# Output projection of a hybrid block on one Trainium2 core: products 6, 7 and 4 accumulate in product 1's PSUM banks, and the transposes between the products move

## The chip, the cores and the metric

The kernel runs on one core of one Trainium2 chip. A core has five engines with a queue each: TensorE (PE in the profile, its weight loads PEld), VectorE (DVE), ScalarE (ACT), GpSimd (POOL) and SyncE (SP, which here only issues DMAs). The engines work in their own order and wait for each other by semaphores. The metric is the device time of one execution in microseconds; the program is compared by the median of several.

## The reference

One layer of a streaming encoder on 512 tokens of 1024 channels: a gated linear attention and a forgetting attention side by side, a gated merge, an output projection with a residual, a gated MLP with a short causal convolution, and a last norm. The part that the change touches is the merge's projection and the norm behind it:

```python
y = sigmoid(g_gla + gate_b[0]) * (o_gla @ w_gla_branch) \
    + sigmoid(g_fox + gate_b[1]) * (o_fox @ w_fox_branch)
x = x + y @ w_out                       # (512, 1024) @ (1024, 1024)
a, val = split(rmsnorm(x, norm_ffn_g) @ w_up, 2)
a = causal_dwconv(a, conv_w, conv_b)
x = x + (gelu(a) * val) @ w_down
return rmsnorm(x, norm_final_g)
```

All of it is float32.

## The kernel before

**Products.** Each float32 product is three TensorE matmuls on rounded parts (`mm3`, L314 to L316: high by high, low by high, high by low). Every weight piece (128 x 1024) is loaded, cast by ScalarE to its high part (`wh`, L280) and subtracted by VectorE to its low part (`wl`, L281), some pieces ahead of TensorE; there are three buffers for each part, so a cast waits until TensorE has left the piece three places back.

**The output projection** `y @ w_out` is done in a Strassen-like scheme: seven products on quarters, each 256 tokens by 512 channels, two weight pieces (r = 0, 1) and 24 matmuls of 128x512. A product fills two PSUM banks, one for each 128 tokens. The order is `OUT`: 1, 5, 2, 3, 6, 7, 4. `out_product` (L1137) issues one. Some weight pieces are sums of blocks: pieces of 6, 7 and 4 arise in place, by accumulating DMAs that GpSimd issues (L288) into the pieces of 5, 3 and 6 as soon as VectorE's split of those has read them. Their tiles are called `zr` (5, 6, 4) and `rawz` (3, 7).

The residual rows `x2[tt][j]` (`x2t` in the profile; tt is the 128-token tile, j the half of the channels) are loaded from x and take the results: `finish_block` (L1151) adds or subtracts two banks (L1154), has ScalarE square the row block for the norm (L1156) and stores it (L1157). Product 1 enters four blocks of the result. It is accumulated with product 2 in its own banks for block (0, 0), and before that copied to SBUF (`ox`, L1200); GpSimd applies the copy to the three other blocks with six additions of 128x512 (L1210). Products 6, 7 and 4 then accumulate in two fresh banks `accy`, which are read after each of them: after 6 for block (0, 1), after 7 for (1, 1), after 4 for (1, 0). Each reading must be over before the next product adds to the bank.

**Transposes.** The MLP wants x by channels. `transpose_half(0)` (L1172, eight 128x128 transposes into two banks) turns block (0, 0) and stands between products 3 and 6; `transpose_later` (L1190, sixteen into four banks) turns blocks (0, 1) and (1, 1) and stands between the two weight pieces of product 4; `transpose_half(1)` stands later, within the first plain MLP products. ScalarE copies the banks out with a scale (L1177, L1191) and casts (L1181, L1192), VectorE subtracts (L1182, L1193).

**Behind the projection** come the first plain products of the up projection (L1234), the sum of squares (L1253), an inverse square root on VectorE (L348 to L358), its spreading over the partitions by TensorE (L412), ScalarE's copy of that (L416) and VectorE's scaling of x (L1297), on which the up projection rests.

The order of an engine's instructions is fixed when the program is built: a scheduler places the recorded instructions by their dependencies, and each queue then runs strictly in that order. PSUM has eight banks in two pools of four, `ps_mm` and `ps_ax`.

Of the kernel before, what the change touches and what calls it, by code (L numbers as in the profile page):

```python
# [9 lines left out]
F32 = mybir.dt.float32  # L10
# [3 lines left out]
AF = mybir.ActivationFunctionType  # L14
# [6 lines left out]
NT = T // P  # L21
D = 1024
KD = D // P
# [10 lines left out]
C_MIX, C_FFN, C_AB, C_OG, C_GB, C_CW, C_CB, C_FB, C_QG, C_KG = 0, 8, 16, 18, 22, 38, 104, 126, 127, 128  # L34
# [16 lines left out]
NCL = 2  # L51
# [30 lines left out]
def hybrid_kernel(ctx: ExitStack, tc, xT, xt, wp, wu, wd, wf, pp, aw2, fing, out):  # L82
    nc = tc.nc
# [218 lines left out]
    def piece():  # L302
        n = taken[0]
        taken[0] += 1
        while len(splits) < min(NP, n + NW + sum(i in spare for i in range(n, n + NW))):
            split_next()
            load_ahead(len(splits))
            for i, b, c in copies_at.get(len(splits) - 1, ()):
                with tc.issue_after(last_load[0].ins):
                    nc.sync.dma_start(wsum[i][:, c], b[:, c])  # L310
        return splits[n]

    def mm3(ps, ah, al, bh, bl, start, stop, **k):
        mm(ps, lhsT=ah, rhs=bh, start=start, stop=False, **k)  # L314
        mm(ps, lhsT=ah, rhs=bl, start=False, stop=False, **k)  # L315
        mm(ps, lhsT=al, rhs=bh, start=False, stop=stop, **k)  # L316
# [62 lines left out]
    def col(c, rows=P):  # L379
        return ppt[:rows, c : c + 1]  # L380
# [5 lines left out]
        out=negm, in_=negm, pattern=[[-1, P]], base=0, channel_multiplier=1, compare_op=ALU.is_ge, fill=-1e30  # L386
# [5 lines left out]
        out=gmask, in_=gmask, pattern=[[1, P]], base=0, channel_multiplier=-1, compare_op=ALU.is_ge, fill=0.0  # L392
# [71 lines left out]
    first = [pmm(), pmm(), pmm(), pmm(), pax()]  # L464
# [16 lines left out]
    for k in range(KD):  # L481
        nc.scalar.activation(out=xh[k], in_=xrs[k], func=AF.Copy, scale=col(C_MIX + k))  # L482
        split_next()
        with tc.issue_after(first_copy[0].ins):
            nc.vector.scalar_tensor_tensor(
                out=xl[k], in0=xrs[k], scalar=col(C_MIX + k), in1=xh[k].bitcast(F32),
# [13 lines left out]
    def last_first(products):  # L500
# [17 lines left out]
        out=gqs, in0=col(C_QG), scalar=FD ** -0.5, in1=col(C_KG), op0=ALU.mult, op1=ALU.mult  # L518
# [32 lines left out]
    for j in range(2):  # L551
# [4 lines left out]
            out=mz[:, j, :], in0=pz, scalar1=col(C_AB + j), scalar2=0.0, op0=ALU.add, op1=ALU.min  # L556
# [11 lines left out]
        out=bz.rearrange("p a b -> p (a b)"), data0=rmask, data1=mz.rearrange("p a b -> p (a b)"),  # L568
# [4 lines left out]
        out=fm, data0=ones[:FH, 0:1].broadcast_to([FH, T]), data1=ft, initial=0.0, op0=ALU.mult, op1=ALU.add,  # L573
# [173 lines left out]
    for j in range(2):  # L747
        pt = pax()
# [29 lines left out]
    for tt in range(NT):  # L778
# [45 lines left out]
    for u in range(2):  # L824
# [251 lines left out]
    for h in range(GH):  # L1076
# [4 lines left out]
            out=zr[h], in0=ogr[h], scalar=col(C_OG + h), in1=zr[h], op0=ALU.mult, op1=ALU.mult  # L1081
# [6 lines left out]
    for c in range(-GAHEAD, KD):  # L1088
# [23 lines left out]
        else:  # L1112
            k = c - KD // 2
# [15 lines left out]
    x2 = [[opool.tile([P, T], F32, tag="ot", name="x2t", bufs=2 * GH) for _ in range(2)] for _ in range(NT)]  # L1129
# [3 lines left out]
    xs = x2pool.tile([P, 2 * KB * H], F32, tag="act2", name="xs")[:, : KD * T].rearrange("p (k t) -> p k t", t=T)  # L1133
    x2h, x2l = xh, xl
    ssq = cpool.tile([P, NT, 2], F32, name="ssq")

    def out_product(p, accs, rs=(0, 1), first=True):  # L1137
        (oh, ol), t0 = oops[p]
        for r in rs:
            wh, wl = held[r] if p == 1 else piece()  # L1140
            for t2 in range(2):
                t = slice(t0 + t2 * P, t0 + (t2 + 1) * P)
                for j in range(2):
                    k = 2 * r + j
                    c = slice(j * 512, (j + 1) * 512)
                    mm3(
                        accs[t2], oh[k][:, t], ol[k][:, t], wh[:, c], wl[:, c], first and k == 0, k == KD // 2 - 1,
                        skip_group_check=not first,
                    )

    def finish_block(i, j, accs, op):  # L1151
        for t2 in range(2):
            x = x2[2 * i + t2][j]
            op(out=x, in0=x, in1=accs[t2])  # L1154
            junk = bpool.tile([P, T], F32, tag="zf", name="junk", bufs=GAHEAD + 1)
            nc.scalar.activation(out=junk, in_=x, func=AF.Square, accum_out=ssq[:, 2 * i + t2, j : j + 1])  # L1156
            nc.scalar.dma_start(x2d[:, 2 * i + t2, j * T : (j + 1) * T], x)  # L1157
# [23 lines left out]
            nc.scalar.copy(out=x2k[0], in_=xs[:, k : k + 2, t])  # L1181
            nc.vector.tensor_sub(out=x2k[1], in0=xs[:, k : k + 2, t], in1=x2k[0].bitcast(F32))  # L1182

    def transpose_later():

        for k in range(KD // 2, KD):
            pt = pax()
            for tt in range(NT):
                c = (k - KD // 2) * P
                nc.tensor.transpose(pt[:, tt * P : (tt + 1) * P], x2[tt][1][:, c : c + P], ident)  # L1190
            nc.scalar.activation(out=xs[:, k], in_=pt, func=AF.Copy, scale=col(C_FFN + k))  # L1191
            nc.scalar.copy(out=x2h[k], in_=xs[:, k])  # L1192
            nc.vector.tensor_sub(out=x2l[k], in0=xs[:, k], in1=x2h[k].bitcast(F32))  # L1193

    accx = [pmm(), pmm()]
    out_product(1, accx)
    ox = []
    for t2 in range(2):
        ox.append(bpool.tile([P, T], F32, tag="sg", name="ox", bufs=2))
        nc.scalar.copy(out=ox[t2], in_=accx[t2])  # L1200
    accz = [pmm(), pmm()]
    out_product(5, accz)
    for t2 in range(2):
        x = x2[2 + t2][1]
        nc.vector.tensor_sub(out=x, in0=x, in1=accz[t2])
    out_product(2, accx, first=False)
    finish_block(0, 0, accx, nc.vector.tensor_add)
    for t2 in range(2):
        for tt, j, op in ((t2, 1, nc.gpsimd.tensor_sub), (2 + t2, 1, nc.gpsimd.tensor_sub), (2 + t2, 0, nc.gpsimd.tensor_add)):
            op(out=x2[tt][j], in0=x2[tt][j], in1=ox[t2])  # L1210
    out_product(3, accz, first=False)
    for t2 in range(2):
        x = x2[t2][1]
        nc.vector.tensor_sub(out=x, in0=x, in1=accz[t2])
    transpose_half(0)
    accy = [pmm(), pmm()]
    out_product(6, accy)
    finish_block(0, 1, accy, nc.vector.tensor_sub)
    out_product(7, accy, first=False)
    finish_block(1, 1, accy, nc.vector.tensor_sub)  # L1220
    out_product(4, accy, rs=(0,), first=False)
    transpose_later()
    out_product(4, accy, rs=(1,), first=False)
    finish_block(1, 0, accy, nc.vector.tensor_add)

# [2 lines left out]
    plain = []  # L1228
# [4 lines left out]
            for ps, (wh, wl) in zip(banks, ws):  # L1233
                mm3(ps, wh[:, c], wl[:, c], x2h[k], x2l[k], k == k0, k == k1)  # L1234

    plain.append((pmm(), pmm()))
    up = (piece(), piece())
    later = range(KD // 2, KD)
    plain_products(plain[0][:1], up[:1], later, later[0], -1)
# [67 lines left out]
    nc.vector.tensor_sub(out=y1, in0=x22, in1=x21)  # L1307
    split_x(5, y1)
    minus_sum(y2, y1, x11)
    plain.append((pmm(), pmm()))  # L1310
    up = (piece(), piece())
    plain_products(plain[1], up, range(KD))
    scale_x(x12, 0)
# [110 lines left out]
    for n, (g, p) in enumerate(steps):  # L1424
# [5 lines left out]
        first = name not in st  # L1430
# [15 lines left out]
        elif p == 4:  # L1446
# [5 lines left out]
            for i, c in enumerate((st["x"], ps)):  # L1452
                for j, k, fs in parts:
                    nc.vector.tensor_mul(
                        out=act[j][:, i, k], in0=halves(c)[:, fs], in1=t0[:, fs, i * H : (i + 1) * H]
# [232 lines left out]
```

## Time and profile before

| | |
|---|---|
| median of 3 runs | 713.47 us (712.8 to 716.25) |
| the profiled execution | 714.62 us |
| its span, first to last instruction | 712.9 us |
| mean granted TensorE clock | 0.992 |
| output projection, products 1 to 4 on TensorE | 324.6 to 373.5 us of the span |

All rows below are from the one profiled execution; their times are in microseconds from the start of its span. A row of the timeline gives start, duration, engine, line, operation, output and inputs, shapes, a count where equal neighbours are merged, and in brackets how long the engine had been idle before and what ended that. Matmul rows overlap, so a matmul's cost is the distance to the next one's start. A row of waits gives the total, the number of times and the longest. The window rows give for a stretch the busy time of each engine with counts, the granted clock as a share of the full one, and how full the DMA engines were.

### The profile page before, as it was taken

How to read it: one execution, taken by the hardware profiler on the slowest of the kernel's cores; microseconds unless marked ns; L12 is line 12 of the kernel's file. 1: busy time of each engine (PE TensorE's matmuls, PEld its weight loads, DVE VectorE, ACT ScalarE, POOL GpSimd, SP SyncE). 2: the span in 40 equal slices, each digit the busy share in tenths (PEclk: the TensorE clock that was granted, in tenths of full speed). 3: DMA queues.
4: the chain of work that ended last, by engine and by line, in shares of the span. 5: the costliest groups of instructions: out<-in, count | busy, mean ns of one | idle time of the engine just before them, and what ended most of it. 6: DMA issues, size and time to landing. Idle time of an engine off the chain costs nothing.

```text
span 712.9 us, 11200 instructions
## 1 busy us (share of the span) xinstructions
PE 695.3 (98%) x4130; PEld 606.2 (85%) x4130; DVE 561.8 (79%) x843; ACT 435.8 (61%) x699; POOL 201.7 (28%) x248
## 2 busy tenths in 40 slices
PE   8999999999999999999899999999999999999996
PEld 6887788787887788888678999999999999888875
DVE  6874888977767675686658998888888889987984
ACT  6487665687967843344556756555565566655653
POOL 6215010225533324335500132243434311000222
PEclk9999999999999999999989999999999999999998
DMA  9658478876666389977747587777777887766643
GB/s 328 252 174 293 96 247 226 294 167 171 163 171 156 90 223 214 264 158 207 160 166 231 124 202 173 168 186 176 188 176 182 205 196 221 269 217 176 192 134 118
DMA packets 44742, 138.19 MB, mean 194 GB/s; under 512 B 5240, under 2 KB 8328, under 8 KB 44560
## 3 DMA queue, kind: packets, MB, share of 16 engines
q1 hardware_dynamic: 30864, 92.85, 38.0%
q0 software_dynamic: 10656, 39.33, 31.0%
q10 hardware_dynamic: 3168, 5.31, 2.1%
q8 instruction: 32, 0.52, 0.3%
q14 instruction: 22, 0.18, 0.1%
HBM read 133.25 MB, written 27.28 MB: 225 GB/s over the span
## 4 chain that ended last, share of the span: by engine, by line
PE 76%; DVE 9%; ACT 5%; DMA 4%; issue 4%; POOL 2%; ACTq 0%; DVEq 0%; POOLq 0%
PE ps_mm L314 18%; PE ps_mm L316 17%; PE ps_mm L315 17%; PE ps_ax L315 6%; PE ps_ax L316 6%; PE ps_ax L314 6%; DVE wl L281 2%; DMA zr<-in_wp_dram 1%; DMA cb<-nct 1%; POOL x2t L1210 1%; DMA rawx<-wsum 1%; DVE ln L949 1%; ACT pr L962 1%; PE ps_pt L971 1%; ACT pr L955 1%
## 5 line engine op out<-in xcount | busy, mean ns | idle before, releaser
L314 PE MATMUL ps_mm<-xh,wh 128*128 128x512 f32 (+1 forms) x312 | 107.4, 346 | 1.2 <-DVE wh L276 0.8
L280 ACT CAST wh<-rawx 128x1024 fp32r<-128x1024 f32 x75 | 76.1, 1014 | 52.4 <-PE ps_mm L315 24.0
L316 PE MATMUL ps_mm<-xh,wl 128*128 128x512 f32 (+1 forms) x312 | 106.6, 343 | 0.0
L315 PE MATMUL ps_mm<-xl,wh 128*128 128x512 f32 (+1 forms) x312 | 106.4, 342 | 0.0
L281 DVE TENSOR_TENSOR wl<-rawx,wh 128x1024 fp32r<-128x1024 f32 x75 | 88.9, 1190 | 14.5 <-ACT wh L280 14.4
L281 DVE TENSOR_TENSOR wl<-raw,wh 128x1024 fp32r<-128x1024 f32 x58 | 78.1, 1349 | 9.1 <-ACT wh L280 8.8
L280 ACT CAST wh<-raw 128x1024 fp32r<-128x1024 f32 x58 | 60.5, 1047 | 28.9 <-PE ps_mm L315 20.4
L314 PEld LDWEIGHTS ps_mm<-xh,wh 128*128 128x128 f32 x312 | 59.1, 190 | 8.3 <-ACT xh L482 1.7
L316 PEld LDWEIGHTS ps_mm<-xh,wl 128*128 128x128 f32 x312 | 59.2, 190 | 7.7 <-DVE wl L277 0.7
L315 PEld LDWEIGHTS ps_mm<-xl,wh 128*128 128x128 f32 x312 | 59.3, 190 | 5.9
L288 POOL DMA_DIRECT2D rawx<-in_wu_dram x30 | 26.1, 869 | 111.2 <-DVE wl L281 106.3
L281 DVE TENSOR_TENSOR wl<-rawz,wh 128x1024 fp32r<-128x1024 f32 x31 | 41.3, 1336 | 18.0 <-ACT wh L280 17.9
L254 POOL TENSOR_TENSOR rawx<-rawx,raw 128x256 f32<-128x256 f32 x32 | 38.2, 1221 | 27.7 <-DMA rawx<-in_wu_dram 27.7
L314 PE MATMUL ps_mm<-xo,wh 128*128 128x256 f32 x160 | 45.5, 284 | 0.0
L315 PE MATMUL ps_mm<-xo,wh 128*128 128x256 f32 x160 | 45.3, 283 | 0.0
L316 PE MATMUL ps_mm<-xo,wl 128*128 128x256 f32 x160 | 45.3, 283 | 0.0
L1331 DVE SCALAR_TENSOR_TENSOR t<-ap,ppt,t 128x512 f32<-128x512 f32 x44 | 43.9, 1051 | 0.0
L280 ACT CAST wh<-rawz 128x1024 fp32r<-128x1024 f32 x31 | 32.4, 1046 | 17.3 <-DMA rawz<-in_wp_dram 6.6
L314 PE MATMUL ps_mm<-wh,xh 128*128 128x512 f32 x108 | 42.8, 398 | 0.1
L314 PE MATMUL ps_mm<-xc,wh 128*128 128x256 f32 (+1 forms) x128 | 42.5, 332 | 0.0
L315 PE MATMUL ps_mm<-xc,wh 128*128 128x256 f32 (+1 forms) x128 | 42.5, 332 | 0.0
L316 PE MATMUL ps_mm<-xc,wl 128*128 128x256 f32 (+1 forms) x128 | 42.4, 331 | 0.0
(471 smaller groups left out, 2046.7 us busy)
## 6 DMA issues: line engine op xcount, KB each, us to landing
rawx<-in_wu_dram POOLq DMA_DIRECT2D x32, 512.0 KB, 6.3
rawz<-in_wp_dram SPq DMA_DIRECT2D x30, 512.0 KB, 5.3
raw<-in_wp_dram SPq DMA_DIRECT2D x22, 512.0 KB, 6.2
wsum<-in_wd_dram SPq DMA_DIRECT2D x20, 512.0 KB, 6.6
rawx<-in_wu_dram SPq DMA_DIRECT2D x20, 512.0 KB, 6.0
raw<-in_wu_dram SPq DMA_DIRECT2D x20, 512.0 KB, 4.6
rawx<-wsum SPq DMA_DIRECT2D x12, 512.0 KB, 4.3
wsum<-in_wd_dram POOLq DMA_DIRECT2D x10, 512.0 KB, 8.6
```

What stands on the lines that cost most here:

```text
L254: nc.gpsimd.tensor_add(out=raws[n][:, c], in0=raws[n][:, c], in1=raws[other][:, c])
L280: nc.scalar.copy(out=hi[:, :m], in_=raw[:, :m])
L281: nc.vector.tensor_sub(out=lo[:, :m], in0=raw[:, :m], in1=hi[:, :m].bitcast(F32))
L288: added[:] = [nc.gpsimd.dma_start(raw, recipes[i][0], accum_op=ALU.add)]
L314: mm(ps, lhsT=ah, rhs=bh, start=start, stop=False, **k)
L315: mm(ps, lhsT=ah, rhs=bl, start=False, stop=False, **k)
L316: mm(ps, lhsT=al, rhs=bh, start=False, stop=stop, **k)
L949: nc.vector.tensor_tensor_reduce(out=ln[:, :n], in0=lg[:, :n], in1=cb[:, CBO[qb] : CBO[qb] + n], scale=-1.0, scalar=3e38, op0=ALU.add, op1 ...
L955: last_exp = nc.scalar.activation(out=pr[:, :n], in_=ln[:, :n], func=AF.Exp, scale=-1.0, bias=nm, accum_out=rs)
L962: nc.scalar.activation(out=pr[:, :n], in_=pr[:, :n], func=AF.Copy, scale=rs)
L971: nc.tensor.transpose(pt[:, c], pr[:, c], ident)
L1331: nc.vector.scalar_tensor_tensor(out=t0[:, i], in0=ap[:, i, w : w + T], scalar=col(C_CW + w * NF + f), in1=t0[:, i], op0=ALU.mult, op1=ALU ...
```

## The change

Product 1 stays in its banks, now called `accy`, and 6, 7 and 4 accumulate onto it, so that its share in blocks (0, 1), (1, 1) and (1, 0) comes by accumulation; GpSimd's six additions go. For block (0, 0) the copy `ox` is added by VectorE (two additions), and product 2 gets two banks of its own from the other pool. `transpose_half(0)` moves behind the reading of product 6; `transpose_later` is split: its first eight transposes, of block (0, 1), stand between products 7 and 4, the other eight, of block (1, 1), between the two pieces of 4, and four banks are held across. The banks of the plain up-projection products are taken in another order, so that the first pair is not the one that product 4 ends in.

```diff
-    def transpose_later():
+    later_banks = []
+
+    def transpose_later(i):
 
         for k in range(KD // 2, KD):
-            pt = pax()
-            for tt in range(NT):
+            if i == 0:
+                later_banks.append(pax())
+            pt = later_banks[k - KD // 2]
+            for tt in range(2 * i, 2 * i + 2):
                 c = (k - KD // 2) * P
                 nc.tensor.transpose(pt[:, tt * P : (tt + 1) * P], x2[tt][1][:, c : c + P], ident)
-            nc.scalar.activation(out=xs[:, k], in_=pt, func=AF.Copy, scale=col(C_FFN + k))
...
+            if i == 1:
+                nc.scalar.activation(out=xs[:, k], in_=pt, func=AF.Copy, scale=col(C_FFN + k))
+                nc.scalar.copy(out=x2h[k], in_=xs[:, k])
+                nc.vector.tensor_sub(out=x2l[k], in0=xs[:, k], in1=x2h[k].bitcast(F32))
+
+    def minus(i, j, accs):
+        for t2 in range(2):
+            x = x2[2 * i + t2][j]
+            nc.vector.tensor_sub(out=x, in0=x, in1=accs[t2])
...
-    accx = [pmm(), pmm()]
-    out_product(1, accx)
+    accy = [pmm(), pmm()]
+    out_product(1, accy)
     ox = []
     for t2 in range(2):
         ox.append(bpool.tile([P, T], F32, tag="sg", name="ox", bufs=2))
-        nc.scalar.copy(out=ox[t2], in_=accx[t2])
+        nc.scalar.copy(out=ox[t2], in_=accy[t2])
     accz = [pmm(), pmm()]
     out_product(5, accz)
     for t2 in range(2):
-        x = x2[2 + t2][1]
-        nc.vector.tensor_sub(out=x, in0=x, in1=accz[t2])
-    out_product(2, accx, first=False)
+        nc.vector.tensor_add(out=x2[t2][0], in0=x2[t2][0], in1=ox[t2])
+    minus(1, 1, accz)
+    accx = [pax(), pax()]
+    out_product(2, accx)
     finish_block(0, 0, accx, nc.vector.tensor_add)
-    for t2 in range(2):
-        for tt, j, op in ((t2, 1, nc.gpsimd.tensor_sub), (2 + t2, 1, nc.gpsimd.tensor_sub), (2 + t2, 0, nc.gpsimd.tensor_add)):
-            op(out=x2[tt][j], in0=x2[tt][j], in1=ox[t2])
     out_product(3, accz, first=False)
-    for t2 in range(2):
-        x = x2[t2][1]
-        nc.vector.tensor_sub(out=x, in0=x, in1=accz[t2])
+    minus(0, 1, accz)
+
+    out_product(6, accy, first=False)
+    finish_block(0, 1, accy, nc.vector.tensor_sub)
     transpose_half(0)
-    accy = [pmm(), pmm()]
-    out_product(6, accy)
-    finish_block(0, 1, accy, nc.vector.tensor_sub)
     out_product(7, accy, first=False)
     finish_block(1, 1, accy, nc.vector.tensor_sub)
+    transpose_later(0)
     out_product(4, accy, rs=(0,), first=False)
-    transpose_later()
+    transpose_later(1)
     out_product(4, accy, rs=(1,), first=False)
     finish_block(1, 0, accy, nc.vector.tensor_add)
...
-    plain.append((pmm(), pmm()))
+    plain_banks = [(pmm(), pmm()) for _ in range(NCL)]
+    plain.append(plain_banks.pop())
...
-    plain.append((pmm(), pmm()))
+    plain.append(plain_banks.pop())
```

The lines of the changed kernel are numbered a little higher: `minus` subtracts at L1203, the additions of `ox` are L1215, `transpose_later`'s transposes L1194, its copies and casts L1196 and L1197; L1154, L1156, L1172, L1177, L280, L281 and L288 keep their numbers.

How the order of instructions moves, at three places. First GpSimd's queue around the projection, as a difference: the `zr` DMA ahead makes a piece of product 6, the two `rawz` DMAs the pieces of 7, the two `zr` DMAs those of 4.

```order
 L288 DMA zr<-in_wp_dram 128x1024
 L1114 TENSOR_TENSOR zf<-zf,zg_1394 128x512
-L1210 TENSOR_TENSOR x2t<-x2t,ox 128x512 x6
 L288 DMA rawz<-in_wp_dram 128x1024 x2
 L288 DMA zr<-in_wp_dram 128x1024 x2
```

The six additions ahead of the DMAs are gone; the DMAs keep their order.

Next VectorE's queue from the splits of product 2's pieces (`raw`) to the reading of product 6's result; `rawz` are the pieces of 3, then of 7, and `zr` those of 6. Before:

```order
L281 TENSOR_TENSOR wl<-raw,wh 128x1024 x2
L1205 TENSOR_TENSOR x2t<-x2t,ps_mm 128x512 x2
L281 TENSOR_TENSOR wl<-rawz,wh 128x1024 x2
L1154 TENSOR_TENSOR x2t<-x2t,ps_mm 128x512 x2
L281 TENSOR_TENSOR wl<-zr,wh 128x1024
L1214 TENSOR_TENSOR x2t<-x2t,ps_mm 128x512
L281 TENSOR_TENSOR wl<-zr,wh 128x1024
L1214 TENSOR_TENSOR x2t<-x2t,ps_mm 128x512
L281 TENSOR_TENSOR wl<-rawz,wh 128x1024
L1182 TENSOR_TENSOR xl<-xs,xh 128x2x256 x2
L281 TENSOR_TENSOR wl<-rawz,wh 128x1024
L1154 TENSOR_TENSOR x2t<-x2t,ps_mm 128x512 x2
```

The same stretch of the changed kernel, where product 2 lies in `ps_ax`:

```order
L1215 TENSOR_TENSOR x2t<-x2t,ox 128x512 x2
L281 TENSOR_TENSOR wl<-raw,wh 128x1024 x2
L1203 TENSOR_TENSOR x2t<-x2t,ps_mm 128x512 x2
L281 TENSOR_TENSOR wl<-rawz,wh 128x1024 x2
L1154 TENSOR_TENSOR x2t<-x2t,ps_ax 128x512 x2
L281 TENSOR_TENSOR wl<-zr,wh 128x1024
L1203 TENSOR_TENSOR x2t<-x2t,ps_mm 128x512
L281 TENSOR_TENSOR wl<-zr,wh 128x1024
L1203 TENSOR_TENSOR x2t<-x2t,ps_mm 128x512
L281 TENSOR_TENSOR wl<-rawz,wh 128x1024 x2
L1154 TENSOR_TENSOR x2t<-x2t,ps_mm 128x512 x2
```

The two additions stand at its head; the subtractions of the transposed block (L1182) no longer stand among the splits of product 7's pieces, but behind.

Last ScalarE's queue behind the projection, from the casts of the last two transposed blocks (`xc`) on; `wh<-rawz` is the cast of the second plain piece of the up projection, and L1156 are the squares of block (1, 0), the last that the sum of squares needs. Before:

```order
L1192 CAST xc_114<-xs 128x512
L1192 CAST xc_115<-xs 128x512
L1156 ACTIVATE junk,ssq<-x2t 128x512
L1157 DMA x2d<-x2t 128x512
L1156 ACTIVATE junk,ssq<-x2t 128x512
```

And in the changed kernel:

```order
L1197 CAST xc_114<-xs 128x512
L1197 CAST xc_115<-xs 128x512
L280 CAST wh<-rawz 128x1024
L1156 ACTIVATE junk,ssq<-x2t 128x512
L1157 DMA x2d<-x2t 128x512
L1156 ACTIVATE junk,ssq<-x2t 128x512
```

The cast of the plain piece, which stood ahead of the transposed blocks' copies, now stands between their last cast and the squares; VectorE's split of that piece likewise stands right ahead of the sum of squares.

More of the change, by code (lines that the diff above doesn't have):

```diff
@@ L1182, in transpose_half @@
             nc.vector.tensor_sub(out=x2k[1], in0=xs[:, k : k + 2, t], in1=x2k[0].bitcast(F32))
-    def transpose_later():
+    later_banks = []
+    def transpose_later(i):
         for k in range(KD // 2, KD):
-            pt = pax()
-            for tt in range(NT):
+            if i == 0:
+                later_banks.append(pax())
+            pt = later_banks[k - KD // 2]
+            for tt in range(2 * i, 2 * i + 2):
                 c = (k - KD // 2) * P
                 nc.tensor.transpose(pt[:, tt * P : (tt + 1) * P], x2[tt][1][:, c : c + P], ident)
-            nc.scalar.activation(out=xs[:, k], in_=pt, func=AF.Copy, scale=col(C_FFN + k))
-            nc.scalar.copy(out=x2h[k], in_=xs[:, k])
-            nc.vector.tensor_sub(out=x2l[k], in0=xs[:, k], in1=x2h[k].bitcast(F32))
-    accx = [pmm(), pmm()]
-    out_product(1, accx)
+            if i == 1:
[8 more added lines that the diff above has]
+    out_product(1, accy)
     ox = []
```

## The prediction

> **What bounds the kernel now.** I read the page first: engine shares, clock in slices, chain.
>
> ```profile
> PE 695.3 (98%) x4130; PEld 606.2 (85%) x4130; DVE 561.8 (79%) x843; ACT 435.8 (61%) x699; POOL 201.7 (28%) x248
> PEclk9999999999999999999989999999999999999998
> PE 76%; DVE 9%; ACT 5%; DMA 4%; issue 4%; POOL 2%; ACTq 0%; DVEq 0%; POOLq 0%
> ```
>
> TensorE is busy 98% of the span and carries 76% of the chain, so a change pays only where TensorE waits or runs slowly. The granted clock dips in one inner slice, the 21st, which covers 356 to 374 us. The waits of TensorE, longest in total first:
>
> ```profile
> PE ps_mm L314 <- DVE x2t L1154: 4.7, 1, 4.7
> PE ps_pt L971 <- ACT pr L962: 1.4, 2, 0.9
> ```
>
> The longest wait of the whole kernel is one of 4.7 us, for the subtraction at L1154; the next is 1.4 us in two parts. Stretches around it (span, busy time and count of PE, PEld, DVE, ACT, POOL, then clock, DMA share, GB/s):
>
> ```profile
> 346.50:352.90 6.40, 6.40 (x33) 5.20 (x31) 2.10 (x3) 1.82 (x4) 2.49 (x3) 1.00 0.94 168
> 352.90:357.70 4.80, 0.14 (x1) 0.02 (x1) 3.83 (x6) 3.92 (x7) 0.00 (x0) 0.92 1.05 217
> 357.70:363.80 6.10, 6.09 (x14) 4.83 (x15) 1.59 (x2) 1.82 (x5) 0.00 (x0) 0.50 0.89 341
> ```
>
> The dip lies here: full clock up to the wait, half of it for 6.1 us behind it, while the DMA engines are full. Why L1154 was late, on VectorE, ScalarE and GpSimd in order of time:
>
> ```profile
> 334.64 10.86 POOL L1210 TENSOR_TENSOR x2t<-x2t,ox 128x512 f32<-128x512 f32 x5 [0.55 <-DMA x2t<-in_xt_dram]
> 338.54 3.46 DVE L281 TENSOR_TENSOR wl<-rawz,wh 128x1024 fp32r<-128x1024 f32 x2
> 345.44 1.77 POOL L288 DMA_DIRECT2D rawz<-in_wp_dram  x2
> 346.57 2.42 POOL L288 DMA_DIRECT2D zr<-in_wp_dram  x2
> 351.08 1.05 ACT L280 CAST wh<-rawz 128x1024 fp32r<-128x1024 f32 x1 [5.98 <-DMA rawz<-in_wp_dram]
> 352.16 1.23 DVE L281 TENSOR_TENSOR wl<-rawz,wh 128x1024 fp32r<-128x1024 f32 x1 [4.30 <-ACT wh L280]
> 355.74 1.23 DVE L281 TENSOR_TENSOR wl<-rawz,wh 128x1024 fp32r<-128x1024 f32 x1 [0.25 <-ACT wh L280]
> 356.88 1.28 DVE L1154 TENSOR_TENSOR x2t<-x2t,ps_mm 128x512 f32<-128x512 f32 x2
> ```
>
> Read backwards. L1154 (p6's result, which must leave its banks before p7 adds to them) starts at 356.88 behind the split of p7's second weight piece (355.74). That piece and the first were made by accumulating DMAs that GpSimd issues in place into p3's pieces. VectorE had finished with those by 342.0 (338.54 + 3.46; the first by about 340.3), but GpSimd was adding until 345.44 and issued then; ScalarE sat 5.98 us until the first landed.
>
> **The change, part by part.** *The wait and the slow clock.* Matmuls by their starts: p5 begins, p6 begins, p6's last, p7's first, p4's first.
>
> ```profile
> 330.10 0.39 PE L314 MATMUL ps_mm<-wh,oh 128*128 128x512 f32 x1
> 347.33 0.48 PE L314 MATMUL ps_mm<-wh,oh 128*128 128x512 f32 x1
> 352.65 0.39 PE L316 MATMUL ps_mm<-wh,ol 128*128 128x512 f32 x1
> 357.71 0.77 PE L314 MATMUL ps_mm<-wh,oh 128*128 128x512 f32 x1 [4.67 <-DVE x2t L1154]
> 366.13 0.39 PE L314 MATMUL ps_mm<-wh,oh 128*128 128x512 f32 x1
> ```
>
> p6, 24 matmuls, took 352.65 + 0.23 - 347.33 = 5.55 us; p7, as many, 366.13 - 357.71 = 8.42. So the wait costs 4.67, and the half clock behind it 8.42 - 5.55 = 2.87.
>
> Will the wait go? Without the six additions GpSimd can issue p7's DMAs as soon as p3's pieces are split, at 340.3 and 342.0 or earlier, against 345.4 and 346.3. The four accumulating zr DMAs and the two rawz ones, from issue to landing:
>
> ```profile
> DMA to landing us min/median/max: 5.3/6.8/11.5
> ```
>
> At the median they land at 347.1 and 348.8. Then casts, which need a free buffer each. The transposes, old place and new, set those times; their rows, and the matmul behind the later sixteen:
>
> ```profile
> 346.54 1.03 PE L1172 MATMUL ps_ax<-ident,x2t 128*128 128x128 f32 x8
> 369.01 1.91 PE L1190 MATMUL ps_ax<-ident,x2t 128*128 128x128 f32 x16
> 370.67 0.48 PE L314 MATMUL ps_mm<-wh,oh 128*128 128x512 f32 x1
> ```
>
> p3 ends and p6 will begin at 346.54, to end at 346.54 + 24 x 0.23 = 352.0; eight transposes take 347.33 - 346.54 = 0.79, so TensorE comes to p7 at 352.8, to its second bank 1.4 later. The two buffers come free at p3's end, 346.5, and in the middle of p6, 349.3. The second piece then takes a cast of 1.05, a split of 1.23 and half of L1154, 0.64: 352.2. No wait, with half a microsecond to spare. In numbers, with 0.2 for semaphores, the wait left is 342.0 + L + 1.05 + 1.23 + 0.64 + 0.2 - 352.8 = L - 7.7 for a landing time L: nothing at the median, 3.8 at 11.5. The 11.5 belongs to the last of four DMAs issued within three microseconds; now their issues spread over 340 to 348, as each split ends. I take nothing.
>
> The slow 2.87 goes with the wait. [...]
>
> *Additions on VectorE.* Six GpSimd additions go; two, L1215, come to VectorE, ahead of p2's splits. Rows of the copy they need, of the place, and of the loads (issue, and time to landing):
>
> ```profile
> 331.83 1.07 ACT L1200 COPY ox<-ps_mm 128x512 f32<-128x512 f32 x2 [1.47 <-issue]
> 333.89 3.53 DVE L281 TENSOR_TENSOR wl<-raw,wh 128x1024 fp32r<-128x1024 f32 x2 [2.49 <-ACT wh L280]
> 325.61 1.39 ACTq L1131 DMA_DIRECT2D x2t<-in_xt_dram  x3
> ...
> x2t<-in_xt_dram ACTq DMA_DIRECT2D x3, 256.0 KB, 4.3
> ```
>
> VectorE idles 2.49 us to 333.89. The copies end at 332.4 and 332.9, two additions at 0.64 end by 333.7: hidden. Without that cover they would cost 1.28. The splits, 1.76 each beside GpSimd's additions against 1.23 alone, get shorter; TensorE does not wait for them, so nothing.
>
> *Accumulation and banks.* p6 now adds to a filled bank and p2 writes a fresh one. p5 (fresh), p2 and p3 (both adding) took 346.54 - 330.10 = 16.44 together, 5.48 each, and p6 (fresh) 5.55, so adding is no slower: within 0.1, and the two swaps cancel. Transposes in three eights rather than eight and sixteen: 3 x 0.79 against 0.79 + 1.66, -0.1 to 0.1. Nothing.
>
> *Behind p4.* Here the new order costs something. First matmul behind p4, last cast, second square, reduction, last step of the inverse root, the matmul that spreads it, and VectorE behind it:
>
> ```profile
> 373.54 0.40 PE L314 MATMUL ps_mm<-xh,wh 128*128 128x512 f32 x1
> 374.00 0.64 ACT L1192 CAST xc<-xs 128x512 fp32r<-128x512 f32 x1
> 375.14 0.64 ACT L1156 ACTIVATE junk<-x2t 128x512 f32<-128x512 f32 x1
> 375.90 0.16 DVE L1253 TENSOR_REDUCE ssq<-ssq 128x4 f32<-128x8 f32 x1 [0.25 <-ACT junk L1156]
> 379.30 0.16 DVE L358 SCALAR_TENSOR_TENSOR rt<-r1w,rt 128x4 f32<-128x4 f32 x1
> 379.96 0.38 PE L412 MATMUL ps_ax<-ident,rt 128*128 128x128 f32 x2
> 383.06 3.50 DVE L1297 TENSOR_TENSOR xs<-xs,rb 128x1024 f32<-128x1024 f32 x3 [2.39 <-ACT rb L416]
> ```
>
> The root is ready at 379.46, TensorE reaches L412 at 379.96: 0.50 to spare. Now a weight cast (1.05) stands between the last cast and the squares, so the reduction comes 1.05 later and TensorE waits 1.05 - 0.50 = 0.55. Bounds: 0, if ScalarE comes through its casts earlier than in the trace, and 1.8, if VectorE's split of that piece (1.23), which also stands ahead of the reduction, is not hidden beside the squares. They take 375.90 - 374.64 = 1.26, as long as the split, so I take 0.55.
>
> *What follows* moves as a whole.
>
> ```profile
> 396.69 1.05 ACT L280 CAST wh<-rawx 128x1024 fp32r<-128x1024 f32 x1 [5.04 <-PE ps_mm L315]
> 403.89 0.39 PE L316 MATMUL ps_ax<-xh,wl 128*128 128x256 f32 x1 [0.34 <-DVE wl L281]
> ```
>
> The first up-projection piece waited for TensorE, not for its load, and TensorE and VectorE meet at 403.89 within 0.34 us; both now come earlier by the same amount.
>
> **Sum.** 4.67 + 2.87 - 0.55 = 7.0 us. The profiled execution took 714.62 (span 712.9), which gives 707.6. It lies 1.15 above the median of the runs, 713.47, so the forecast for a median is 706.5.
>
> **Rivals.**
>
> *A late landing keeps part of the wait.* For it: DMA share 0.94 to 1.05 in these stretches, and a wait that starts at L = 7.7 with 6.8 the median. Against it: the four no longer pile up. At 9.6, half way to the worst, 1.9 remain: 708.4. At the worst, 3.8 remain: 710.3, or 713.2 if the clock falls too. Where it falls is bounded by rows: not at 1.66 us without ordinary matmuls (the sixteen transposes, after which the stretch keeps clock 1.00), certainly at 4.67.
>
> ```profile
> 363.80:373.70 9.90, 9.90 (x52) 8.19 (x51) 6.62 (x8) 7.35 (x14) 0.96 (x2) 1.00 0.15 53
> ```
>
> [...]
>
> *The additions were not the cause:* the DMAs wait for something else and the stall stays, 713.5. Against: the issue at 345.44 follows the last addition without a gap, and VectorE was done with the tiles at 342.0.
>
> *Slower:* L1215 now heads VectorE's queue, and every split for p2 stands behind it; if the x2 rows it adds to land late, TensorE stops in p2. Issued from 325.61 to 327.0 with 4.3 us to landing, they are there by 331.3. The first split then ends at 333.9 + 1.23 = 335.1, half a microsecond before the trace's (335.65, and TensorE did not wait); so a landing costs from 333.1 on, a microsecond each. To be 3.6 slower than now it must eat 7.0 + 3.6 = 10.6: a wait of 7.7 plus 2.87 of slow clock, a landing at 340.8, some 14 us behind the issue. It would give 717.1.
>
> **How the numbers follow.** Forecast, 705.9 (no wait at L412) to 707.8 (1.8 there): 0.76. Late landing, 708 to 713: 0.17. Not the cause: 0.04. Slower: 0.03. About 0.5%, 3.6 us, is what a measurement of this kernel can tell from no change. Faster by more means below 709.9: the forecast and over half of the late landings, 0.87. Within: the rest of these and the third case, 0.10. Slower: 0.03. The range goes from 704.8 (no new wait, and the 0.7 us by which the fastest run of before lies under its median, with 0.4 of splits and banks) to 710.3, the late landing without the clock.
>
> **What would show it.** Right: no wait of TensorE for L1154 over 0.5 us; p7 in about 5.5 us at clock 1.00; the two rawz DMAs issued by 342; L412 waiting about half a microsecond for the root. Wrong: a wait at p7's first matmul, with ScalarE waiting for rawz in front of it (late landing); a wait in p2 behind L1215 (slower); or TensorE stopping in the up projection for weights, the gain given back there.

## The result, and the profile after

Against the kernel before on the same chip the changed kernel took **707.6 us** (median of 6 runs, 706.07 to 709.74), the kernel before 713.98 (6 runs, 712.8 to 716.25): ratio **0.9908**, 95% interval 0.9881 to 0.9934. The profiled execution took 706.07, its span 704.3 at a mean clock of 0.997. Two executions in the experiments, one of 851.44 us (transposes alone) and one of 1764.02 (three idle operations), are far slower than the others of their kernels and are left out of the medians below.

The page of the changed kernel: engine shares, clock in slices, chain.

```profile
PE 691.6 (98%) x4130; PEld 604.0 (86%) x4130; DVE 561.2 (80%) x845; ACT 435.8 (62%) x699; POOL 190.1 (27%) x242
PEclk9999999999999999999999999999999999999998
PE 82%; DVE 9%; ACT 4%; issue 2%; DMA 1%; ACTq 0%; DVEq 0%
```

The dip of the clock in the 21st slice is gone, and TensorE carries 82% of the chain, not 76%; GpSimd has left it. The waits of TensorE, longest first, and the one new one:

```profile
PE ps_ax L366 <- DVE ones L375: 1.3, 1, 1.3
...
PE ps_ax L412 <- DVE rt L358: 0.6, 1, 0.6
```

No wait of TensorE names L1154 any more. The longest wait of TensorE left is one of 1.3 us at L366, which the kernel before has too. The stretches that hold product 6 with the eight transposes, and product 7 (columns as in the prediction: engines' busy time, clock, DMA share, GB/s):

```profile
344.40:351.40 7.00, 7.00 (x36) 5.86 (x35) 5.49 (x7) 2.66 (x3) 0.86 (x1) 1.00 0.98 181
351.40:357.00 5.60, 5.60 (x28) 4.58 (x27) 2.61 (x4) 4.98 (x12) 0.00 (x0) 1.00 0.97 316
```

TensorE is busy throughout, at full clock, and product 7 takes 5.6 us where it took 8.4. Why, in the order of the chain that was late before: GpSimd's issues of product 7's pieces, their casts, splits, and the reading of product 6.

```profile
337.56 0.88 POOL L288 DMA_DIRECT2D rawz<-in_wp_dram  x1 [10.41 <-DVE wl L281]
339.78 0.86 POOL L288 DMA_DIRECT2D rawz<-in_wp_dram  x1 [1.35 <-DVE wl L281]
348.11 1.05 ACT L280 CAST wh<-rawz 128x1024 fp32r<-128x1024 f32 x1 [1.63 <-PE ps_mm L316]
349.19 1.23 DVE L281 TENSOR_TENSOR wl<-rawz,wh 128x1024 fp32r<-128x1024 f32 x1 [1.45 <-ACT wh L280]
350.33 1.28 DVE L1154 TENSOR_TENSOR x2t<-x2t,ps_mm 128x512 f32<-128x512 f32 x2
351.43 0.48 PE L314 MATMUL ps_mm<-wh,oh 128*128 128x512 f32 x1
```

GpSimd now sits idle until VectorE has split product 3's pieces, and issues at once: what releases the DMAs is VectorE, not the last addition. The second cast waited for a free buffer, not for the load (1.63 us, released by a matmul), so the landing is hidden: 7.1 us behind the issue at 339.78, at 346.9, 1.2 ahead of the cast. The last row is product 7's first matmul: no idle time in brackets.

Two profiles start at different times, so for comparisons I count from product 1's first matmul (324.64 before, 323.30 after); up to there the programs are alike, and in the profiles read here that point lies between 323.2 and 326.4. From it to the first plain product (the first matmul `xh,wh` behind product 4) were 48.90 us before and 41.00 after; to the first matmul of the next section, which reads `xo`, 72.76 and 65.78, that is 6.98 less; to the span's end 388.26 and 381.00.

### The profile page after: what moved, and what is told of

It is laid out like the page before. It is cut to its first block, busy times and chain, and to the rows that moved or that the text cites. A ratio compares the mean times of both kernels' runs of the same rounds, so it can differ in the third digit from the quotient of the medians.

```text
span 704.3 us, 11193 instructions
## 1 busy us (share of the span) xinstructions
PE 691.6 (98%) x4130; PEld 604.0 (86%) x4130; DVE 561.2 (80%) x845; ACT 435.8 (62%) x699; POOL 190.1 (27%) x242
## 4 chain that ended last, share of the span: by engine, by line
PE 82%; DVE 9%; ACT 4%; issue 2%; DMA 1%; ACTq 0%; DVEq 0%
PE ps_mm L314 19%; PE ps_mm L316 19%; PE ps_mm L315 19%; PE ps_ax L315 6%; PE ps_ax L316 6%; PE ps_ax L314 6%; DVE wl L281 3%; PE ps_pt L971 1%; DMA rawx<-wsum 1%; PE ps_po L995 1%; PE ps_lg L945 1%; PE ps_po L994 1%; PE ps_lg L946 1%; DVE xs L1307 1%; DMA ppt<-in_pp_dram 1%
## 5 line engine op out<-in xcount | busy, mean ns | idle before, releaser
L280 ACT CAST wh<-rawx 128x1024 fp32r<-128x1024 f32 x75 | 76.1, 1014 | 52.6 <-PE ps_mm L315 24.0
L281 DVE TENSOR_TENSOR wl<-rawx,wh 128x1024 fp32r<-128x1024 f32 x75 | 89.1, 1190 | 14.7 <-ACT wh L280 14.7
L281 DVE TENSOR_TENSOR wl<-raw,wh 128x1024 fp32r<-128x1024 f32 x58 | 77.4, 1335 | 6.4 <-ACT wh L280 6.3
L280 ACT CAST wh<-raw 128x1024 fp32r<-128x1024 f32 x58 | 60.5, 1047 | 31.7 <-PE ps_mm L315 19.8
L288 POOL DMA_DIRECT2D rawx<-in_wu_dram x30 | 26.1, 869 | 109.8 <-DVE wl L281 104.2
L281 DVE TENSOR_TENSOR wl<-rawz,wh 128x1024 fp32r<-128x1024 f32 x31 | 40.4, 1304 | 15.1 <-ACT wh L280 15.1
L280 ACT CAST wh<-rawz 128x1024 fp32r<-128x1024 f32 x31 | 32.5, 1048 | 17.3 <-issue 7.3
```

The lines of the kernel that those rows point to most:

```text
L280: nc.scalar.copy(out=hi[:, :m], in_=raw[:, :m])
L281: nc.vector.tensor_sub(out=lo[:, :m], in0=raw[:, :m], in1=hi[:, :m].bitcast(F32))
L288: added[:] = [nc.gpsimd.dma_start(raw, recipes[i][0], accum_op=ALU.add)]
```

## The experiments

Distances on TensorE, from each profile, in us. "p7 to plain" goes from product 7's first matmul to the first plain one: at full clock it is 12.87. A dash: not measured.

| kernel | median | ratio to before (95%) | wait L1154 | p7 to plain | wait L412 | p1 to plain |
|---|---|---|---|---|---|---|
| before, first profile | 713.98 | 1 | 4.67 | 15.83 | none | 48.90 |
| before, second profile | - | - | 4.25 | 14.60 | none | 47.25 |
| changed | 707.6 | 0.9908 (0.9881 to 0.9934) | none | 12.87 | 0.61 | 41.00 |
| changed, again | 707.04 | 0.9919 (0.9898 to 0.994) | none | 12.86 | 0.65 | 40.99 |
| transposes alone | 713.2 | 1.0003 (0.9986 to 1.002) | 3.34, 3.62 | 14.46, 14.49 | 0.65, 0.66 | 46.18, 46.48 |
| accumulation alone | 706.66 | 0.9912 (0.9892 to 0.9932) | 0.38 | 12.87 | none | 41.65 |
| additions on VectorE | 709.07 | 0.9944 (0.9924 to 0.9964) | 0.40 | 13.00 | none | 43.25 |
| six idle, ahead | 712.11 | 0.9984 (0.9963 to 1.0004) | 3.02 | 14.49 | 0.61 | 46.05 |
| five idle, ahead | - | - | 0.48 | 12.84 | 0.63 | 41.82 |
| three idle, ahead | 707.09 | 0.9922 (0.9901 to 0.9944) | - | - | - | - |
| six idle, behind | 708.01 | 0.9928 (0.9905 to 0.9952) | none | 12.87 | 0.68 | 40.99 |
| later transposes whole | 706.74 | 0.9918 (0.9892 to 0.9944) | none | 12.86 | 0.64 | 40.98 |
| spreading later | 707.3 | 0.9919 (0.9899 to 0.994) | none | 12.87 | 0.66 | 41.00 |

**The two halves of the change.** First the changed kernel once more beside them.

> The changed kernel once more beside the others, to have its time on the same chip: 707.6, with a wait of 0.6 us at L412 and none for L1154.

Then before's arithmetic with the transposes at the new places:

```diff
     out_product(3, accz, first=False)
...
-    transpose_half(0)
     accy = [pmm(), pmm()]
     out_product(6, accy)
     finish_block(0, 1, accy, nc.vector.tensor_sub)
+    transpose_half(0)
     out_product(7, accy, first=False)
     finish_block(1, 1, accy, nc.vector.tensor_sub)
+    transpose_later(0)
     out_product(4, accy, rs=(0,), first=False)
-    transpose_later()
+    transpose_later(1)
```

> The kernel before with its arithmetic and its six GpSimd additions, and only the transposes moved as in the change. Queue theory (the six additions delay the accumulating DMAs for p7): the two rawz DMAs are still issued right behind the additions, the second lands some 7 us later, and TensorE waits for L1154 in front of p7 for about 3.5 to 4 us, eight transposes less than the 4.67 of before; the clock may or may not fall to half behind it. The new order at the tail costs 0.55 at L412. Median 713 with the slow clock, 710.5 without. Order theory (the copies and subtractions of the transposed block between p7's splits held L1154 back): the whole gain, 707.6, no wait for L1154.

And the changed kernel with all transposes at the old places (the reverse of this diff):

> The changed kernel with all transposes at their old places, so only the accumulation in p1's banks (and no GpSimd additions). Queue theory: the rawz DMAs are issued at the splits of p3, 4 us or more ahead of the place they had; L1154 is held only by ScalarE's copies of the transposed block ahead of the second cast, a wait of at most 0.6 us; clock 1.00; no cast between the last transposed block and the squares, so no wait at L412. Median about 707. Order theory: the wait of 4.7 us and the slow clock stay, 713.5.

Accumulation alone gives the whole gain, the moves alone nothing that can be measured. In the profile of the moves alone the waits of TensorE are, longest first,

```profile
PE ps_mm L314 <- DVE x2t L1154: 3.3, 1, 3.3
...
PE ps_ax L412 <- DVE rt L358: 0.6, 1, 0.6
```

and in that of the accumulation alone

```profile
PE ps_mm L314 <- DVE x2t L1154: 0.4, 1, 0.4
```

The wait for L1154 is shorter with the moves (3.3 and 3.6, against 4.7 and 4.3), but not because the eight transposes fill a part of it, as was expected: TensorE has the same work ahead of product 7 in either order and comes to it 28.4 us behind product 1's start in all four profiles. L1154 itself is earlier. ScalarE's copies of the transposed block no longer stand between product 7's two casts, so the second cast waits for its load alone, 28.67 behind product 1's start, where before, behind the copies, it began at 30.03. First before, then the moves alone:

```profile
354.67 1.04 ACT L280 CAST wh<-rawz 128x1024 fp32r<-128x1024 f32 x1
```

```profile
352.85 1.04 ACT L280 CAST wh<-rawz 128x1024 fp32r<-128x1024 f32 x1 [1.66 <-DMA rawz<-in_wp_dram]
```

Against that stands the 0.6 at L412. The accumulation alone has it the other way round, 0.4 at L1154 and none at L412. The two sides cancel: from product 1 to the matmul that reads `xo` the moves alone take 70.98 and 71.26, the second profile of before, whose clock loss is as short, 71.12; the accumulation alone takes 65.54, the changed kernel 65.78.

**Is it the six additions, or where they run?** Before with its additions on VectorE, and nothing else:

```diff
-        for tt, j, op in ((t2, 1, nc.gpsimd.tensor_sub), (2 + t2, 1, nc.gpsimd.tensor_sub), (2 + t2, 0, nc.gpsimd.tensor_add)):
+        for tt, j, op in ((t2, 1, nc.vector.tensor_sub), (2 + t2, 1, nc.vector.tensor_sub), (2 + t2, 0, nc.vector.tensor_add)):
```

> The kernel before with one edit: the six additions of ox on VectorE in place of GpSimd; banks and transposes as before. Queue theory: as with the accumulation alone, about 707, since six additions of 0.64 us find room on VectorE ahead of p3's end; the wait for L1154 at most 1 us. If the accumulation itself (fewer instructions, fewer readings of memory) were what pays: 713.5, or slower by the 3.8 us on VectorE.

Freeing GpSimd's queue brings most of the gain with all the arithmetic kept; the gain is 2.4 us smaller than that of accumulation alone (709.07 against 706.66). VectorE and TensorE in product 2 of this kernel show a good half of the difference:

```profile
334.57 1.40 DVE L1210 TENSOR_TENSOR x2t<-x2t,ox 128x512 f32<-128x512 f32 x2 [0.55 <-DMA x2t<-in_xt_dram]
335.89 2.35 DVE L281 TENSOR_TENSOR wl<-raw,wh 128x1024 fp32r<-128x1024 f32 x2
337.16 0.50 PE L315 MATMUL ps_mm<-wl,oh 128*128 128x512 f32 x1 [1.16 <-DVE wl L281]
```

The additions wait for rows of x still being loaded, product 2's splits stand behind them in VectorE's queue, and TensorE stops for 1.16 us: product 2 takes 6.99 from its first matmul to product 3's, not 5.55. Up to the first plain product the two profiles differ by 1.60 (43.25 against 41.65); the rest was not traced. That is the mechanism of the prediction's slower rival, here with a load that arrives some 10 us behind product 1's start.

**How much GpSimd work, and on which side of the DMA issues?** The changed kernel with work for GpSimd that nothing uses, n = 3, 5 or 6 times behind the reading of product 2, which puts it ahead of the `rawz` DMAs; the output stays the same:

```diff
     finish_block(0, 0, accx, nc.vector.tensor_add)
+    for i in range(n):
+        nc.gpsimd.tensor_sub(out=ox[i % 2], in0=ox[i % 2], in1=ox[i % 2])
```

> The changed kernel with three idle subtractions of 128x512 on GpSimd (ox minus itself, used by nothing) ahead of the rawz DMAs. Theory 'queue' (the additions cost time only by standing in front of the DMA issues in GpSimd's queue): they end about 15 us behind the start of product 1, when VectorE has just split product 3's first piece; the issues move by less than 1 us, no wait of TensorE for L1154 over 0.6, time as the changed kernel's, 707 +-0.7. Theory 'sharing' (GpSimd's additions cost by slowing VectorE beside them, in proportion to their number): half of the 6 us comes back, 710. Theory 'order of the transposes': 707.

> The changed kernel with six such subtractions. Theory 'queue': they end about 21 us behind the start of product 1, as the six additions of before did (20.8), the rawz DMAs are issued then, TensorE waits 3.3 to 3.7 us for L1154 and the clock falls behind it: from product 1's start to the first plain product 46 us where the changed kernel has 41.0, time 712 to 713. Theory 'sharing': the same 712 to 713, but with TensorE waiting for VectorE in many places and not for L1154 behind rawz. Theory 'arithmetic' (the gain is in the work that went, not in the queue): 707 to 708.

> The changed kernel with five idle subtractions ahead of the rawz DMAs. With six they ended 18.9 us behind the start of product 1, at 1.72 each, and TensorE waited 3.0. With five they end at 17.2. Theory 'queue': the wait is 3.0 - 1.7 = 1.3, and the clock does not fall behind it, since the shortest wait behind which it fell so far is 3.0: 42.5 us from product 1 to the first plain product (41.0 without, 46.05 with six). If the clock falls behind a wait of 1.3 too, 44.

Then six such operations that read a result of product 6, so that they stand behind the `rawz` and `zr` DMAs in the same queue:

```diff
     finish_block(0, 1, accy, nc.vector.tensor_sub)
+    for i in range(6):
+        nc.gpsimd.tensor_sub(out=ox[i % 2], in0=x2[i % 2][1], in1=x2[i % 2][1])
```

> The changed kernel with six subtractions of 128x512 on GpSimd that nothing uses (a row block of x2 minus itself into ox), which stand behind the rawz and zr DMAs in GpSimd's queue, not ahead of them. Theory 'queue': the issues keep their times, no wait of TensorE for L1154 over 0.6, 707 +-0.7, against 712.1 with six ahead. Theory 'sharing': VectorE beside them is slowed as with six ahead, 711 to 713.

Three ahead cost nothing that can be measured, 707.09 (three runs, 706.93 to 707.95), by the times alone. Six ahead bring back almost the whole loss, six behind none of it. GpSimd's queue with six ahead, the late cast and the wait:

```profile
333.45 10.35 POOL L1222 TENSOR_TENSOR ox<-ox 128x512 f32<-128x512 f32 x6 [4.75 <-DVE x2t L1215]
343.74 1.78 POOL L288 DMA_DIRECT2D rawz<-in_wp_dram  x2
353.37 1.04 ACT L280 CAST wh<-rawz 128x1024 fp32r<-128x1024 f32 x1 [1.95 <-DMA rawz<-in_wp_dram]
```

```profile
PE ps_mm L314 <- DVE x2t L1154: 3.0, 1, 3.0
```

With five ahead, from the same views:

```profile
331.81 8.36 POOL L1222 TENSOR_TENSOR ox<-ox 128x512 f32<-128x512 f32 x5 [4.74 <-DVE x2t L1215]
340.11 0.88 POOL L288 DMA_DIRECT2D rawz<-in_wp_dram  x1
341.55 0.86 POOL L288 DMA_DIRECT2D rawz<-in_wp_dram  x1 [0.56 <-DVE wl L281]
349.15 1.05 ACT L280 CAST wh<-rawz 128x1024 fp32r<-128x1024 f32 x1 [2.62 <-DMA rawz<-in_wp_dram]
352.20 0.47 PE L314 MATMUL ps_mm<-wh,oh 128*128 128x512 f32 x1 [0.48 <-DVE x2t L1154]
```

The second issue comes 1.85 us later than in the changed kernel (18.33 behind product 1's start, not 16.48), and it is no longer the queue but VectorE's split, itself slower beside GpSimd's work (two of them in 3.84 us, 1.92 each, against 1.22 and 1.23 in the changed kernel), that it waits for. It lands 7.5 us behind the issue; the wait is 0.48, not the 1.3 expected, because most of the delay goes into the slack that the landing had in the changed kernel. With six, the first issue comes 18.89 behind the start and the second within another microsecond; the landing takes 8.9 us, the cast behind it starts 2.6 later than with five (28.52 against 25.93), and the wait is 2.5 longer. So the cost has a threshold: up to five operations nearly all of the queue's delay is covered; the sixth, 1.72 us long, costs 2.5 of waiting and 1.6 of slow clock. With six behind, GpSimd was busy as well,

```profile
351.22 7.46 POOL L1226 TENSOR_TENSOR ox<-x2t 128x512 f32<-128x512 f32 x6 [4.09 <-DVE x2t L1154]
```

and nothing waited for it: its median, 708.01, lies within the scatter of the changed kernel, and every distance on TensorE is that of the changed kernel to 0.1. "Sharing" would have had to cost there too, though these six ran at 1.24 us each beside a VectorE busy for 3.9 of the 6.8 us from 351.22 to 358.00, against 1.72 for the six ahead (1.67 for the five, beside a VectorE without a gap from 334.23 on), so this is a weaker test than the threshold.

**The slow clock.** A second profile each of the kernel before and of the moves alone.

> The kernel before, unchanged, looked at a second time. Its timed executions list a mean granted clock of 0.992 to 0.993 in 7 of 17 and 0.995 to 0.997 in 10; the profiled one had 0.992. Theory 'two lengths': the slow stretch behind the wait lasts about 6.5 us in the one kind and 3.3 in the other, so that with 0.996 here product 7 takes about 7 us and not 8.4. Theory 'always 2.87': product 7 takes 8.4 whatever the clock listed.

> Before with the transposes at the new places alone, looked at a second time. In its first profile, from product 1's start to the span's end took 385.3 us against 388.3 of before, but its median was no better than that of before. If the moves gain something where the clock fall is long (theory 'shorter slow stretch'), this profile shows again a wait of about 3.3 us, a slow stretch of about 3.3 us and 46 us from product 1 to the first plain product; if the first profile was a lucky one, 47.5 to 49.

Behind a wait of 4.25 us product 7's stretch lost 14.60 - 12.87 = 1.73, where the first profile had lost 15.83 - 12.87 = 2.96. Windows of one microsecond (span, busy time and count of TensorE, clock, DMA share, GB/s), first from the first profile of before, then from the second, then from six idle ahead:

```profile
356.00:357.00 1.00, 0.00 (x0) 0.99 1.05 209
357.00:358.00 1.00, 0.29 (x1) 0.50 1.07 279
363.00:364.00 1.00, 1.00 (x4) 0.60 0.07 25
```

```profile
356.00:357.00 1.00, 1.00 (x3) 0.66 1.03 299
359.00:360.00 1.00, 1.00 (x5) 0.63 1.04 401
```

```profile
356.00:357.00 1.00, 0.59 (x2) 0.75 1.05 262
359.00:360.00 1.00, 1.00 (x4) 0.54 1.00 401
```

The clock is 1.00 or 0.50 in these profiles, with a mean between the two only where a window holds a fall or a rise, so a mean m in a microsecond means 2 x (1 - m) us of it at half speed. Then the clock was halved from 356.32 to 359.74 in the second profile (3.42 us), from 356.50 to 359.92 with six ahead (3.42), but from 356.98 to 363.80 in the first (6.82, twice as long). In the two short cases TensorE was at work again when the clock fell (from 356.00 and 356.41 on); in the long one it came back 0.73 us after the fall, at 357.71. The two profiles of the moves alone have the short form (14.46 and 14.49; 3.42 us in each, to 359.74 and 359.42), and there too TensorE was back first (355.90 and 355.81, falls at 356.32 and 356.00). Which form came up went, in these five profiles, with whether TensorE was at work again before the clock fell; only one of them shows the long form, and no run shows what makes it twice as long. The clock falls once more at the very end, in the first and the second profile here,

```profile
708.00:709.00 1.00, 0.00 (x0) 0.78 0.00 0
```

```profile
707.00:708.00 1.00, 0.00 (x0) 0.95 0.82 313
```

that is at 708.56 and 707.90, in both 351.58 us behind the first fall; what sets that distance no run shows. In the changed kernel's profile the one fall is such a fall at the end, at 700.36 (0.68 from 700 to 701).

The timed executions of the kernel before list a mean clock each. Of 43 in the three comparisons behind the experiments, 20 had 0.994 or less (median 713.88) and 23 more than that (712.42). The two profiles, at 0.992 and 0.997, show the long and the short form. The changed kernel, without a fall in the projection, lists 0.997 to 0.999; 3.42 us at half speed take an estimated 0.0024 off that and 6.82 take 0.0048, which gives 0.995 to 0.997 for the short form and 0.992 to 0.994 for the long one. That the other executions divide in this way is thus worked out from their clocks, not traced.

**The new wait at L412.** The changed kernel with `transpose_later` whole again between product 4's pieces, `transpose_half(0)` left at its new place:

```diff
     finish_block(1, 1, accy, nc.vector.tensor_sub)
-    transpose_later(0)
     out_product(4, accy, rs=(0,), first=False)
-    transpose_later(1)
+    transpose_later()
```

> The changed kernel with transpose_later in one piece of sixteen between product 4's pieces, as before; transpose_half(0) stays behind product 6. Theory 'the weight cast among the tail makes the wait at L412': that cast stays where it is, the wait at L412 stays 0.6 and the time is that of the changed kernel, 707 +-0.5. Theory 'the split transposes make it': in the kernel with all transposes at their old places TensorE did not wait at L412 but 0.4 for L1154; here it would wait for neither, and the time is 0.4 to 0.6 lower, 706.3.

The wait stays. ScalarE's tail in this kernel:

```profile
367.29 0.64 ACT L1192 CAST xc<-xs 128x512 fp32r<-128x512 f32 x1
367.81 1.07 ACT L280 CAST wh<-rawz 128x1024 fp32r<-128x1024 f32 x1
368.76 0.65 ACT L1156 ACTIVATE junk<-x2t 128x512 f32<-128x512 f32 x1
```

The weight cast of 1.07 us still stands between the last `xc` and the squares. Whether the later transposes are split or whole does not matter. This kernel and accumulation alone, which has no such wait, differ in the place of `transpose_half(0)` alone, so its move is the cause. The median of 706.74 is not below the changed kernel's by more than the scatter. Last, the spreading of the root placed further back in the plain products:

```diff
-    plain_products(plain[0], up, range(1), -1, KD // 2 - 1)
+    plain_products(plain[0], up, range(2), -1, KD // 2 - 1)
...
-    plain_products(plain[0], up, range(1, KD // 2), -1, KD // 2 - 1)
+    plain_products(plain[0], up, range(2, KD // 2), -1, KD // 2 - 1)
```

> The changed kernel with the spreading of the inverse root (L412) placed behind two pieces' worth of plain products instead of one. Theory 'TensorE's wait at L412 is worth its length': it goes, 0.6 lower, 706.4. Theory 'VectorE's scaling is what is late': the spread copy comes as late or later, TensorE waits further back for the same, 707 to 707.6.

This run does not answer its question: only the last four of the eight small matmuls moved (from 50.17 to 51.57 behind product 1's start), the first, which waits, stood where it had stood and waited 0.66. What it shows is another thing:

```profile
377.37 0.59 ACT L416 COPY rb<-ps_ax 128x512 f32<-128x512 f32 x1 [4.21 <-PE ps_ax L412]
397.56 0.39 PE L316 MATMUL ps_ax<-xh,wl 128*128 128x256 f32 x1 [0.52 <-DVE wl L281]
```

The spread copy starts 52.21 behind product 1, 1.4 later than in the changed kernel (50.82), and the later stop of TensorE grew from 0.34 to 0.52: VectorE's scaling has about 1.2 us to spare.

No version tried beats the changed kernel by more than the scatter.

## Why the prediction was right

- **The stall of 4.67.** Gone, as said, and by the mechanism named: GpSimd issues product 7's DMAs when VectorE has split product 3's pieces. On before's scale (product 1 at 324.64) the issues are at 338.90 and 341.12, predicted 340.3 and 342.0 "or earlier"; TensorE reaches product 7 at 352.77, predicted 352.8. Of the 5.2 us by which the second issue moved (346.3 before), 1.2 are not the queue's: VectorE's splits, without GpSimd's additions beside them (1.22 and 1.23 us, against 3.46 for the two), were over at 340.8 and not 342.0. That the queue behind the additions is the cause is shown from three sides: the same additions on VectorE free it, idle work ahead of the issues brings most of the wait back with the sixth operation, and the same amount behind them does not.
- **The landing.** No landing was late: the casts in the changed kernel waited for buffers, and the second piece landed 7.1 us behind its issue, within the 7.7 of the forecast's bound. The forecast had half a microsecond to spare; with five idle operations, where the issue is 1.85 later, 0.48 of waiting was left, so the slack was real and small. The bound L - 7.7 counts 1.05 + 1.23 + 0.64 + 0.2 = 3.12 from the second cast to product 7's first matmul, 0.2 of it for semaphores; in the profile of before these were 3.04 (354.67 to 357.71). It is written for an issue at 342.0; with five, on the same scale, it is 1.0 later, which with L = 7.5 gives 0.8, and 0.48 was measured: TensorE itself came to product 7 0.4 later than in the changed kernel.
- **The slow clock, 2.87.** Right for the profiled execution, 2.96 by the distances (its slow stretch was 6.82 us and not 6.1: the clock had fallen 0.73 before TensorE came back), but over-sized as a term for the median: in the second profile of before it was 1.73, and about half of the executions list the clock that goes with it. This is the part of the forecast that a single profile could not carry, and the wait was a draw as well. With the means of the two profiles, 4.46 for the wait and 2.35 for the clock, the sum is 4.46 + 2.35 - 0.55 = 6.3 off the median of 713.47: 707.2, against 706.5 forecast and 707.6 and 707.0 measured. No run shows what sets the two lengths, 3.42 and 6.82. The forecast bounds where the clock falls by 1.66 us of transposes, which takes these as idle; no run shows that. Of the waits for L1154 the longest without a fall was 0.48 us, the shortest with one 3.02.
- **The new wait, 0.55.** Measured 0.61 to 0.68, for the reason given, a weight cast of 1.07 between the last `xc` and the squares. The prediction put it down to the new order in general; the runs narrow it to `transpose_half(0)`.
- **Sum.** 7.0 predicted for the profiled execution; from product 1 to the matmul that reads `xo` the profiles differ by 6.98. That they agree so closely is partly luck: term by term it is 4.94 up to product 7 (4.67 forecast), 2.96 behind it (2.87), and 0.92 lost behind the first plain product (0.55).
- **Costed at nothing.** Accumulating onto a full bank and the bank swaps: nothing to see. Product 6 takes 5.44 us onto product 1's sums in the changed kernel and 5.44 into fresh banks with the moves alone; product 2 takes 5.55 into fresh banks and 5.55 onto product 1's. L1215 on VectorE was hidden, but six additions there were not (1.16 us in product 2), so the cover was there for two and not for six.
- **Rivals.** "Additions not the cause" falls with three runs. The late landing and the slower case did not occur; the mechanism of the latter did, at a small size, with the additions on VectorE.
- **The moves of the transposes** had no term of their own but the -0.55. Alone they are worth nothing measurable, 1.0003 (0.9986 to 1.002), because they bring L1154 forward and the root back by about as much.

## What to carry to other kernels

GpSimd, which here both computes and issues DMAs, delayed its loads by what stood ahead of them in its queue (the second issue came at 346.3, on the same scale at 341.1 without the additions): where a load is late, look first at its issue time and at what ended just before it. What such work cost here had a threshold, the slack of the load (0.48 us of waiting with five operations, 3.02 with six), and beyond it the clock fell as well (1.6 us more). Moving work on an engine that would have waited anyway gained nothing by itself here (the moves alone, 1.0003): look at what it lets come earlier. A clock loss read from one profile is one draw of several: before it goes into a sum for a median, set it beside the mean clocks of the other executions.

## What the runs showed of the hardware

- The granted clock stayed at 0.50 for 3.42 us (four profiles) or for 6.82 (one) behind waits of 3.0 to 4.7 us for L1154; behind waits of 0.4 and 0.5 us for L1154 it stayed 1.00.
- An idle GpSimd subtraction of 128x512 took 1.24 us (six in 7.46) beside a VectorE busy for 3.9 of 6.8 us, 1.67 (five in 8.36) beside one without a gap and 1.72 (six in 10.35) in the same place; one VectorE split took 2.06 us in the run with five, against 1.23 in the changed kernel.
